# Weight sums of one output product made in earlier pairs, with their loads and stores on ScalarE's queue

## The chip, the cores and the metric

The kernel runs on 1 core of one Trainium2 chip. Times are device microseconds (us) of one execution. The times before are three runs, 1965.34, 1966.95 and 1966.96 us, median 1966.95 us. The engines are named as in the profile: PE (TensorE matmuls) and PEld (its weight loads), DVE (VectorE), ACT (ScalarE), POOL (GpSimd) and SP (SyncE, which here only issues DMAs).

## The reference

One decoder layer over 512 tokens of width 2048, all in float32. The change touches the weights of the output product `mix @ w_out`.

```python
h = rms_norm(x, norm1_g)
proj = h @ w_in                                   # 2048 x 6160
qa, ka, va, ra, ga, qb, kb, vb = split(proj)
out_a = gla_mixer(qa, ka, va, ra, log_g(ga), onorm_g)      # 4 heads
out_b = dilated_mixer(norm(qb), norm(kb), vb, rel_bias)    # 8 heads
mix = concatenate([out_a, out_b])
x = x + mix @ w_out                               # 2048 x 2048
h2 = rms_norm(x, norm2_g)
x = x + (silu(h2 @ w_gate) * (h2 @ w_up)) @ w_down
```

## The kernel before

Every large product is made by a scheme with seven multiplications in place of eight (Strassen-Winograd) on 2 x 2 blocks. A **pair** is two blocks of 512 output columns that are made together. A pair runs through seven products in the order P1, P5, P6, P3, P7, P2, P4, each over four groups g0 to g3 of 512 input rows. One product of one group is an **item**, so a pair has 28 items. The weights of a group come as four quarters a, b, c, d of 256 rows x 512 columns (512 KB each, `load_quarter`, line 222). P1, P3 and P2 take a, d and c as they are. P5, P6, P7 and P4 take the differences b-a, d-a, d-b and c-a (with the a of that moment), which DVE makes in place (`Pair.source`, line 256): 16 sums of 128 x 1024 in a pair.

In an item, ACT rounds the weights to the high part `wh` (line 331, a "cast"), DVE makes the remainder `wl` (line 335), and PE multiplies: eight matmuls with `wh`, four with `wl` (line 367, 128x512 each). Two buffers each hold `wh` and `wl`, and twelve (`wpool`) hold quarters, so ACT can be at most one item ahead of PE.

The order of the pairs: a hand-ordered first pair (lines 435 and before, columns qa and ka); then `pairs[0]` (va), `pairs[1]` (qb0, kb0), `pairs[2]` (vb), `pairs[3]` (qb1, kb1), `pairs[4]` (the gate), two pairs of the output product (here **out(0)** and out(1)), eleven pairs of gate and up, six of down. The mixers run as background generators, which `p.step()` advances once per item. The left operands of out(0) (`AA`, `AS` in the trace, made at lines 174, 175 and 1251 to 1255) come out of the mixers only while the gate pair and out(0) already run. At the end of the gate pair, line 1178 makes the last gated values (`cr`), which PE transposes at line 1129.

All loads and stores are issued on SP's queue, but for three small ones on ACT's queue at the start. In `pairs[0]` SP also issues line 628, the load `rep_d<-bias_d`, which repeats the bias tables in memory: 2560 KB in one DMA.

Only the first pair is recorded under `tc.manual_schedule(engines=ordered)`. For all that comes after, the framework sorts each engine's instructions by itself, so an instruction's place on its engine is not the place where the source calls it. Each engine then works through its queue in that order, and an instruction that waits holds all behind it. Each DMA of SP and ACT gets one of eight completion counters in turn, and is issued only when the DMA before it on the same counter has landed.

Of the kernel before, what the change touches and what calls it, by code (L numbers as in the profile page):

```python
# [10 lines left out]
F32 = mybir.dt.float32  # L11
# [3 lines left out]
ALU = mybir.AluOpType  # L15
# [3 lines left out]
P = 128  # L19
# [14 lines left out]
SINGLE = {"P1": "a", "P3": "d", "P2": "c"}  # L34
SUMS_OF = {"P5": "ba", "P6": "da", "P7": "db", "P4": "ca"}
# [72 lines left out]
def block_kernel(ctx: ExitStack, tc: tile.TileContext, ins, out):  # L108
    nc = tc.nc
    x, w_in, w_out, w_gate, w_up, w_down = (  # L110
        ins[n] for n in ("x", "w_in", "w_out", "w_gate", "w_up", "w_down")
    )
# [33 lines left out]
    load = nc.sync.dma_start  # L146
# [89 lines left out]
    class Pair:  # L236


        def __init__(self, op, rows, w1, w2, final, step, scale=None, before=None):
            self.op, self.rows, self.w1, self.w2 = op, rows, w1, w2  # L240
            self.final, self.step, self.scale, self.before = final, step, scale, before
            self.q, self.dst, self.held = {}, {}, {}

        def quarter(self, name, g):
# [5 lines left out]
        def source(self, prod, g):  # L250

            if prod in SINGLE:
                return self.quarter(SINGLE[prod], g)
            one, two = SUMS_OF[prod]
            src = self.quarter(two, g)
            nc.vector.tensor_tensor(src, self.quarter(one, g), src, op=ALU.subtract)  # L256
            return src
# [50 lines left out]
        def end(self, prod):  # L308
            src = self.dst[prod]
            if prod in ("P1", "P5", "P6"):  # L310
                self.held[prod] = self.seeds(src, int(prod == "P5"))
            elif prod == "P4":
                later(1, lambda: self.final(1, 0, None, src), hold=True)
            else:
                which = {"P3": "P6", "P7": "P5", "P2": "P1"}[prod]
                self.close(self.held[which], src, *CLOSES[prod])

    def stream(pairs):

# [184 lines left out]
    def later(units, fn, hold=False):  # L504

        deferred.append([units, fn, hold])
# [20 lines left out]
    def finish(ready):  # L527

        tries = 0
        while not ready():  # L530
            tries += 1
            assert tries < 100
            run_soon()
            try:
                next(background[0])
            except StopIteration:
                background.pop(0)

    def paced(counts):
        counts = iter(counts)  # L540
        return lambda: step(next(counts, 1))

    def rate(*stretches):


        owed = [0.0]
        rates = iter([r for n, r in stretches for _ in range(n)])

        def go():
            owed[0] += next(rates, stretches[-1][1])  # L550
            n = owed[0] if owed[0] > 0.3 else 0
            owed[0] = min(owed[0] - (step(n) or 0.0), 1.0)

        return go
# [79 lines left out]
    row_scale = lambda half, m: rs1[:, 2 * half + m : 2 * half + m + 1]  # L634
# [464 lines left out]
    order = (2, 3, 0, 1)  # L1099

    def final_proj(n1, n2):
        def final(half, which, tiles, acc_):
            if tiles is None:
                tiles = emitted(acc_, lambda m: row_scale(half, m))
            name = (n1, n2)[which]
            dst = proj[name]
            for m in range(2):
                r = half * 256 + m * P
                put = lambda r=r, m=m: store(dst[r : r + P, :], tiles[m])
                if name[:2] in ("qb", "kb"):  # L1110
# [183 lines left out]
    opm = Operand(4)  # L1294
    pairs = []

    def pair(*args, **kw):
        pairs.append(Pair(*args, **kw))

    pair(opx, rows_in, col(1536), col(1024), final_proj("va1", "va0"), rate((22, 1), (6, 0.6)),  # L1300
         row_scale, before=lambda: background.extend([gates(), bias_tables()]))
    flow = rate((90, 0.41))
    pair(opx, rows_in, col(3088), col(4112), final_proj("qb0", "kb0"), flow, row_scale)
    pair(opx, rows_in, col(5648), col(5136), final_proj("vb1", "vb0"), flow, row_scale)
    pair(opx, rows_in, col(3600), col(4624), final_proj("qb1", "kb1"), flow, row_scale)
    pair(opx, rows_in, col(2048), col(2560), final_gate, rate((5, 0.6), (23, 1.05)), row_scale)


    rows_mix = [(1024 + 256 * g, 256 * order[g]) for g in range(4)]
# [36 lines left out]
    def final_out(second):  # L1346
        rest_of = {}

        def ahead(half, which):
            tok = 1 - half  # L1350
            rest_of[half, which] = residual_loads(
                [2 * tok, 2 * tok + 1], 512 * (2 * second + which),
                lambda t, c: x[t * P : (t + 1) * P, c : c + 512],
            )

        def final(half, which, tiles, acc_):
            tok = 1 - half
            rows = [2 * tok, 2 * tok + 1]
            ch = 2 * second + which
            tiles = residual(tiles, acc_, rest_of.pop((half, which)))  # L1360
            for m in range(2):
                t = rows[m]
                store(x1_d[t][:, 512 * ch : 512 * ch + 512], tiles[m])
                jk = work("st", (P, DV), bufs=2).bitcast(mybir.dt.bfloat16)
                nc.scalar.activation(
                    jk, tiles[m], AF.Square, accum_out=ss2[:, t, ch : ch + 1]
                )
            if second:
                turn = scaled_store(tiles, rows, tok, xn_d[2 * ch : 2 * ch + 2], 4 * ch)

                def rest():
                    turn()
                    if which == 1 and half == 1:
                        background.append(early_jobs(opn, (2, 3), tops, False))
                        background.append(late_jobs(opn, ((2, 3),), tops, bots, False))

                later(2, rest)
                if which == 0 and half == 1:
                    output_scales()
            elif which == 0 and half == 1:  # L1380
                nc.vector.tensor_tensor(part2, ss2[:, :, 0], ss2[:, :, 1], op=ALU.add)
# [35 lines left out]
        turn()  # L1417
        yield

    ocol = lambda c: w_out[:, c : c + 512]  # L1420
# [98 lines left out]
    for j in range(11):  # L1519
        c = slice(512 * j, 512 * j + 512)  # L1520
# [32 lines left out]
    for i in range(3):  # L1553
        g0 = 4 * i
        rows_d = [(512 * (g0 + g), 512 * (g0 + g) + 256) for g in range(opd[i].groups)]
        for np_ in range(2):
            c = 1024 * np_
# [4 lines left out]
                before=(lambda i=i: background.append(down_jobs(i + 1))) if lead else None,  # L1562
# [46 lines left out]
```

## Time and profile before

| | |
|---|---|
| runs | 1965.34, 1966.95, 1966.96 us, median 1966.95 |
| profiled execution, its own time | 1968.84 us |
| its span in the profile | 1967.1 us |
| PE busy | 1927.6 us (98%) |
| DVE busy | 1653.7 us (84%) |
| ACT busy | 1093.8 us (56%) |
| DMA queue q1 (SP) | 358.72 MB, 57.6% of 16 engines |

The page gives busy time by engine, the span in 40 slices, the DMA queues, the chain of work that ended last, and groups of like instructions. A row of the timeline gives the start in us, the duration, engine and line, the tiles written and read, how many instructions it merges, and in brackets the idle time before it and who ended it. A row of the windows gives a stretch, its length, busy us of PE, PEld, DVE, ACT and POOL, the granted TensorE clock, the share of the DMA engines in use, and GB/s.

### The profile page before, as it was taken

To read this page: it belongs to the slowest core of one execution; us is meant where nothing else is said; L and a number is where in the kernel's file an instruction comes from. 1 tells how busy PE (TensorE), PEld (TensorE's weight loads), DVE (VectorE), ACT (ScalarE), POOL (GpSimd) and SP (SyncE) were. 2 spreads that over 40 slices of the span, in tenths; PEclk is the share of its full clock that TensorE was granted. 3 is DMA by queue.
4 is the path that set the end of the run, shared out by engine and by line. 5 is a ranking of instruction groups with operands and counts; after the bars stand their busy time and mean duration, and the time that the engine had idled before them with its cause. 6 is when DMAs were issued, how large, how long until landed. Compare 5 with 4: busy or idle time off the path is not lost.

```text
span 1967.1 us, 25785 instructions
## 1 busy us (share of the span) xinstructions
PE 1927.6 (98%) x9226; PEld 1670.9 (85%) x9226; DVE 1653.7 (84%) x1850; ACT 1093.8 (56%) x1600; POOL 60.9 (3%) x81
## 2 busy tenths in 40 slices
PE   8999999999999999999999999999999999999998
PEld 7888888888878877888888888888888888888887
DVE  8997787868789889878878878878879989989987
ACT  8554564566766766545545445545446646546443
POOL 0000230010000000000000000000000000000000
PEclk9999999999999999999999999999999999999999
DMA  8447455463766684554554553554555865855662
GB/s 278 141 162 266 119 171 170 134 200 124 221 213 202 215 288 152 177 167 133 178 170 127 179 163 127 176 164 130 172 163 168 299 203 185 310 183 175 236 214 75
DMA packets 237114, 360.45 MB, mean 183 GB/s; under 512 B 18246, under 2 KB 96783, under 8 KB 236984
## 3 DMA queue, kind: packets, MB, share of 16 engines
q1 hardware_dynamic: 236776, 358.72, 57.6%
q8 instruction: 72, 1.18, 0.3%
q14 instruction: 58, 0.48, 0.1%
q10 hardware_dynamic: 208, 0.08, 0.0%
HBM read 296.59 MB, written 64.51 MB: 184 GB/s over the span
## 4 chain that ended last, share of the span: by engine, by line
PE 75%; DVE 8%; DMA 5%; issue 3%; ACT 2%; POOL 0%; SPq 0%; DVEq 0%; ACTq 0%
PE acc L367 71%; DVE wl L335 3%; DVE wa L256 2%; PE bank L1129 1%; DVE AS L175 1%; PE bank L987 1%; DMA q<-in_x 1%; DMA xn_d<-oT 1%; ACT wh L331 1%; DMA q<-y_d 0%; DVE seed L294 0%; PE bank L1019 0%; DVE seed L1334 0%; DMA r<-xn_d 0%; DMA wc<-in_w_down 0%
## 5 line engine op out<-in xcount | busy, mean ns | idle before, releaser
L367 PE MATMUL acc<-wh,AS 128*128 128x512 f32 x3008 | 712.5, 380 | 0.6 <-ACT wh L331 0.5
L367 PEld LDWEIGHTS acc<-wh,AS 128*128 128x128 f32 x3008 | 569.8, 190 | 82.3 <-ACT wh L331 1.8
L331 ACT CAST wh<-wa 128x1024 fp32r<-128x1024 f32 x376 | 394.0, 1048 | 392.4 <-PE acc L367 363.0
L367 PE MATMUL acc<-wh,AA 128*128 128x512 f32 x2256 | 535.0, 380 | 0.0
L335 DVE TENSOR_TENSOR wl<-wa,wh 128x1024 fp32r<-128x1024 f32 x376 | 456.3, 1217 | 69.2 <-ACT wh L331 43.6
L367 PEld LDWEIGHTS acc<-wh,AA 128*128 128x128 f32 x2256 | 427.4, 190 | 61.4 <-ACT wh L331 0.9
L367 PE MATMUL acc<-wl,AS 128*128 128x512 f32 x1504 | 395.3, 385 | 9.7 <-DVE wl L335 9.5
L367 PEld LDWEIGHTS acc<-wl,AS 128*128 128x128 f32 x1504 | 279.4, 189 | 62.0 <-DVE wl L335 21.0
L367 PE MATMUL acc<-wl,AA 128*128 128x512 f32 x1128 | 298.1, 387 | 7.9 <-DVE wl L335 7.7
L367 PEld LDWEIGHTS acc<-wl,AA 128*128 128x128 f32 x1128 | 209.6, 190 | 41.5 <-DVE wl L335 12.4
L331 ACT CAST wh<-wb 128x1024 fp32r<-128x1024 f32 x94 | 98.5, 1049 | 129.7 <-PE acc L367 127.8
L331 ACT CAST wh<-wc 128x1024 fp32r<-128x1024 f32 x94 | 98.4, 1047 | 111.5 <-PE acc L367 101.7
L331 ACT CAST wh<-wd 128x1024 fp32r<-128x1024 f32 x94 | 98.5, 1048 | 105.8 <-PE acc L367 102.3
L256 DVE TENSOR_TENSOR wa<-wc,wa 128x1024 f32<-128x1024 f32 x94 | 114.4, 1221 | 46.2 <-DMA wc<-in_w_gate 25.1
L335 DVE TENSOR_TENSOR wl<-wc,wh 128x1024 fp32r<-128x1024 f32 x94 | 114.5, 1218 | 35.6 <-ACT wh L331 35.6
L335 DVE TENSOR_TENSOR wl<-wd,wh 128x1024 fp32r<-128x1024 f32 x94 | 114.3, 1219 | 34.9 <-ACT wh L331 28.2
L335 DVE TENSOR_TENSOR wl<-wb,wh 128x1024 fp32r<-128x1024 f32 x94 | 113.6, 1216 | 5.5 <-ACT wh L331 5.5
L256 DVE TENSOR_TENSOR wb<-wd,wb 128x1024 f32<-128x1024 f32 x94 | 114.3, 1216 | 1.1 <-DMA wd<-in_w_in 0.6
L256 DVE TENSOR_TENSOR wa<-wb,wa 128x1024 f32<-128x1024 f32 x94 | 113.6, 1218 | 0.8
L256 DVE TENSOR_TENSOR wa<-wd,wa 128x1024 f32<-128x1024 f32 x94 | 112.8, 1215 | 0.1
L298 DVE SCALAR_TENSOR_TENSOR seed<-acc,rs,seed 128x512 f32<-128x512 f32 x96 | 70.4, 745 | 24.9 <-PE acc L367 24.9
L282 ACT ACTIVATE seed<-acc,rs 128x512 f32<-128x512 f32 x96 | 60.6, 681 | 1.4 <-PE acc L367 0.8
(303 smaller groups left out, 1365.1 us busy)
## 6 DMA issues: line engine op xcount, KB each, us to landing
wa<-in_w_gate SPq DMA_DIRECT2D x44, 512.0 KB, 3.9
wb<-in_w_up SPq DMA_DIRECT2D x44, 512.0 KB, 4.3
wd<-in_w_up SPq DMA_DIRECT2D x44, 512.0 KB, 4.3
wc<-in_w_gate SPq DMA_DIRECT2D x44, 512.0 KB, 3.7
wc<-in_w_in SPq DMA_DIRECT2D x28, 512.0 KB, 3.9
wa<-in_w_in SPq DMA_DIRECT2D x24, 512.0 KB, 5.1
wb<-in_w_in SPq DMA_DIRECT2D x24, 512.0 KB, 6.0
wd<-in_w_in SPq DMA_DIRECT2D x24, 512.0 KB, 5.9
```

What stands on the lines that cost most here:

```text
L175: nc.vector.tensor_tensor(a[:, :, 1, :], src, a[:, :, 0, :].bitcast(F32), op=ALU.subtract)
L256: nc.vector.tensor_tensor(src, self.quarter(one, g), src, op=ALU.subtract)
L282: nc.scalar.activation(halves(t), unfolded(src[m]), AF.Copy, scale=self.scale(half, m))
L298: nc.vector.scalar_tensor_tensor(halves(seed[m]), unfolded(src[m]), self.scale(half, m), halves(seed[m]), op0=ALU.mult, op1=ALU.add,)
L331: nc.scalar.copy(high[k], sources[k])
L335: nc.vector.tensor_tensor(low[k], sources.pop(k), high[k].bitcast(F32), op=ALU.subtract)
L367: nc.tensor.matmul(p.dst[prod][m], a[:, jj, hl, m * P : (m + 1) * P], folded(w[:, jj, :]), start=fresh and g == 0 and len(terms) == 2 and ...
L987: nc.tensor.matmul(lp[:, :n], qh[:, b * P : (b + 1) * P], kh[:, :n], start=True, stop=True)
L1129: nc.tensor.transpose(bk[:, jj, m * P : (m + 1) * P], tiles[m][:, f : f + P], ident)
```

## The change

The 16 sums of out(0) are no longer made in out(0). A generator `weight_sums` makes them in `pairs[0]` to `pairs[2]` in eight blocks (group g, half j): four loads of 128 x 512 (256 KB) from `w_out` into `rpool` (four buffers), four sums of 128 x 512 on DVE, and four stores of 256 KB into DRAM tiles `P5_g_d`, `P7_g_d`, `P6_g_d`, `P4_g_d`. Loads and stores are issued by `nc.scalar.dma_start`, that is on ACT's queue. `beside` advances the plan one step per item; a block starts every nine items from item 12 on. In out(0), `source` loads a finished sum (512 KB, tile `ws`) with SP, so that out(0) has 28 loads of 512 KB instead of 16.

```diff
         def source(self, prod, g):
 
             if prod in SINGLE:
-                return self.quarter(SINGLE[prod], g)
+                t = self.quarter(SINGLE[prod], g)
+                if self.sums:
+                    self.q.pop((SINGLE[prod], g))
+                return t
+            if self.sums:
+                t = wpool.tile([P, 2, 512], F32, name=nm("ws"), tag="w")
+                load(t, self.sums[prod, g])
+                return t
...
+    def weight_sums(rows, w1, w2, sums):
+        tt = nc.vector.tensor_tensor
+        plan = {}
+
+        def at(group, fn):
+            plan.setdefault(group, []).append(fn)
+
+        def block(start, g, j):
+            t = {}
+
+            def fetch(name):
+                r0 = rows[g][0 if name in "ab" else 1] + P * j
+                t[name] = rpool.tile([P, 512], F32, name=nm("r"), tag="r")
+                nc.scalar.dma_start(t[name], (w1 if name in "ac" else w2)[r0 : r0 + P, :])
+
+            def less(dst, one, two):
+                tt(t[dst], t[one], t[two], op=ALU.subtract)
+
+            def put(prod, name):
+                nc.scalar.dma_start(sums[prod, g][:, j, :], t[name])
+
+            at(start, lambda: fetch("a"))
+            at(start, lambda: fetch("b"))
+            at(start + 1, lambda: fetch("d"))
+            at(start + 2, lambda: fetch("c"))
+            for i, (dst, one, two, prod) in enumerate(
+                (("a", "b", "a", "P5"), ("b", "d", "b", "P7"), ("d", "d", "a", "P6"),
+                 ("c", "c", "d", "P4"))
+            ):
+                at(start + 4 + i, lambda dst=dst, one=one, two=two: less(dst, one, two))
+                at(start + 5 + i, lambda prod=prod, dst=dst: put(prod, dst))
+
+        for i in range(8):
+            block(12 + 9 * i, i // 2, i % 2)
+        for n in range(max(plan) + 1):
+            for fn in plan.get(n, ()):
+                fn()
+            yield
...
+    early_sums = weight_sums(rows_mix, ocol(0), ocol(512), out_sums)
+    pair(opx, rows_in, col(1536), col(1024), final_proj("va1", "va0"),
+         beside(rate((22, 1), (6, 0.6)), early_sums),
          row_scale, before=lambda: background.extend([gates(), bias_tables()]))
     flow = rate((90, 0.41))
+    flowing = beside(flow, early_sums)
-    pair(opx, rows_in, col(3088), col(4112), final_proj("qb0", "kb0"), flow, row_scale)
-    pair(opx, rows_in, col(5648), col(5136), final_proj("vb1", "vb0"), flow, row_scale)
+    pair(opx, rows_in, col(3088), col(4112), final_proj("qb0", "kb0"), flowing, row_scale)
+    pair(opx, rows_in, col(5648), col(5136), final_proj("vb1", "vb0"), flowing, row_scale)
...
-    pair(opm, rows_mix, ocol(0), ocol(512), final_out(0), paced([1] * 28))
+    pair(opm, rows_mix, ocol(0), ocol(512), final_out(0), paced([1] * 28), sums=out_sums)
```

The changed program, as built, has this order of instructions in `pairs[0]` (st and ld are DMA stores and loads of the plan, the number in brackets is the block, and each line is in order on its queue):

```
ACT  cast P3 g3 | st P6(0), ld a(1), ld b(1) | cast P7 g0 | st P4(0), ld d(1) | cast P7 g1 | ld c(1)
     cast P7 g2 | st P5(1) | cast P7 g3 | st P7(1), st P6(1), ld a(2) | cast P2 g0 | st P4(1), ld b(2)
     cast P2 g1 | ld d(2), ld c(2) | cast P2 g2
     st P5 P7 P6 P4 (2), ld a b d c (3), st P5 P7 P6 P4 (3), ld a b d c (4), ... , st P5 P7 P6 P4 (7)
     cast P2 g3 | cast P4 g0 ...
DVE  wl P2 g1 | sums 1, 2 of (2) | wl P2 g2 | sums 3, 4 of (2) | the 20 sums of (3) to (7)
     weight sum of P4 g3 | wl P2 g3 ...
SP   rep_d | va store, va store, load c of P2 g3 ("wc"), va store, va store, T load, T load, v load | loads of pairs[1]
```

Waits in it that the dependencies of the data do not show: st P6(1) has the counter of `rep_d`; the two va stores, the wc load and the next va store on SP have the counters of ld a(7), b(7), d(7) and c(7). A load of a block goes into the buffer whose store of the block before must have landed (a after P5, b after P7, d after P6, c after P4). In `pairs[1]` to `pairs[4]` the order on every engine is that of before. In out(0) the remaining instructions of DVE, ACT and SP are sorted anew.

More of the change, by code (lines that the diff above doesn't have):

```diff
@@ L236, in block_kernel, with __init__ @@
     class Pair:
-        def __init__(self, op, rows, w1, w2, final, step, scale=None, before=None):
+        def __init__(self, op, rows, w1, w2, final, step, scale=None, before=None, sums=None):
             self.op, self.rows, self.w1, self.w2 = op, rows, w1, w2
             self.final, self.step, self.scale, self.before = final, step, scale, before
+            self.sums = sums
             self.q, self.dst, self.held = {}, {}, {}
@@ L537, in finish, with beside, both @@
                 background.pop(0)
+    def beside(go, gen):
+        def both():
+            go()
+            next(gen, None)
+        return both
     def paced(counts):
@@ L1298, in pair @@
         pairs.append(Pair(*args, **kw))
-    pair(opx, rows_in, col(1536), col(1024), final_proj("va1", "va0"), rate((22, 1), (6, 0.6)),
+    ocol = lambda c: w_out[:, c : c + 512]
+    rows_mix = [(1024 + 256 * g, 256 * order[g]) for g in range(4)]
+    out_sums = {
+        (prod, g): dram([P, 2, 512], f"{prod}_{g}_d") for prod in SUMS_OF for g in range(4)
+    }
+    early_sums = weight_sums(rows_mix, ocol(0), ocol(512), out_sums)
+    pair(opx, rows_in, col(1536), col(1024), final_proj("va1", "va0"),
+         beside(rate((22, 1), (6, 0.6)), early_sums),
          row_scale, before=lambda: background.extend([gates(), bias_tables()]))
     flow = rate((90, 0.41))
-    pair(opx, rows_in, col(3088), col(4112), final_proj("qb0", "kb0"), flow, row_scale)
-    pair(opx, rows_in, col(5648), col(5136), final_proj("vb1", "vb0"), flow, row_scale)
+    flowing = beside(flow, early_sums)
+    pair(opx, rows_in, col(3088), col(4112), final_proj("qb0", "kb0"), flowing, row_scale)
+    pair(opx, rows_in, col(5648), col(5136), final_proj("vb1", "vb0"), flowing, row_scale)
     pair(opx, rows_in, col(3600), col(4624), final_proj("qb1", "kb1"), flow, row_scale)
     pair(opx, rows_in, col(2048), col(2560), final_gate, rate((5, 0.6), (23, 1.05)), row_scale)
-    rows_mix = [(1024 + 256 * g, 256 * order[g]) for g in range(4)]
     x1_d = [dram([P, D], f"x1_d{t}") for t in range(4)]
@@ L1418, in first_columns @@
         yield
-    ocol = lambda c: w_out[:, c : c + 512]
     def output_scales():
```

## Prediction

> **What bounds the kernel now.** I read the page's head first, then the windows, then the timeline of PE and DVE in the stage that the change relieves, then that of ACT, PE and SP in the stage that it loads.
>
> ```profile
> span 1967.1 us, 25785 instructions
> PE 1927.6 (98%) x9226; PEld 1670.9 (85%) x9226; DVE 1653.7 (84%) x1850; ACT 1093.8 (56%) x1600; POOL 60.9 (3%) x81
> ```
>
> PE is the bound, with 39.5 us of idle time in the whole span. Less work on DVE gains only where PE waits for DVE. Two windows and the timeline show that out(0) is such a place.
>
> ```profile
> 500.00:600.00 100.00, 90.90 (x464) 76.05 (x462) 79.17 (x121) 65.93 (x121) 0.00 (x0) 0.98 0.66 206
> 570.00:580.00 10.00, 7.92 (x31) 6.50 (x32) 8.86 (x13) 8.57 (x15) 0.00 (x0) 0.83 0.59 187
> ```
> ```profile
> 559.20 1.04 PE L1129 MATMUL bank<-mats,seed 128*128 128x128 f32 x8
> ...
> 560.93 1.89 PE L367 MATMUL acc<-wh,AA 128*128 128x512 f32 x8
> ...
> 570.11 1.13 PE L367 MATMUL acc<-wl,AA 128*128 128x512 f32 x4 [1.40 <-DVE wl L335]
> 573.05 0.44 PE L1129 MATMUL bank<-mats,cr 128*128 128x128 f32 x2 [1.81 <-DVE cr L1178]
> ...
> 574.84 3.02 PE L367 MATMUL acc<-wh,AA 128*128 128x512 f32 x8
> ...
> 578.57 1.89 PE L367 MATMUL acc<-wh,AS 128*128 128x512 f32 x8
> ...
> 604.05 1.89 PE L367 MATMUL acc<-wh,AS 128*128 128x512 f32 x8
> ...
> 645.50 1.89 PE L367 MATMUL acc<-wh,AA 128*128 128x512 f32 x8
> ```
>
> out(0) begins at 560.93. Its items 1 to 4 (P1) reach to 578.57, items 5 to 12 (P5, P6) to 604.05, and the last 16 to 645.50. The last 16 take 41.45 us, 2.59 each, without loss. At that pace P5 and P6 would take 20.7 us and not 25.48 (4.8 lost). P1 takes 17.64 where four items (10.4) and eight transposes of line 1129 (1.04 for such eight at 559.20) need 11.4: 6.2 lost. So 11.0 us can be won in out(0), and no more. What PE waits for there is DVE:
>
> ```profile
> 562.17 1.23 DVE L256 TENSOR_TENSOR wa<-wb,wa 128x1024 f32<-128x1024 f32 x1
> 563.43 1.23 DVE L256 TENSOR_TENSOR wb<-wd,wb 128x1024 f32<-128x1024 f32 x1
> ...
> 570.57 1.22 DVE L256 TENSOR_TENSOR wa<-wb,wa 128x1024 f32<-128x1024 f32 x1
> 571.70 0.69 DVE L1253 TENSOR_TENSOR r<-r,qT 128x512 f32<-128x512 f32 x1
> 572.30 1.29 DVE L1178 TENSOR_TENSOR cr<-cr,og 128x512 f32<-128x512 f32 x2
> ...
> 580.11 1.22 DVE L256 TENSOR_TENSOR wa<-wb,wa 128x1024 f32<-128x1024 f32 x1
> 581.24 0.68 DVE L175 TENSOR_TENSOR AS<-r,AS 128x512 fp32r<-128x512 f32 x1
> 581.85 1.22 DVE L335 TENSOR_TENSOR wl<-wa,wh 128x1024 fp32r<-128x1024 f32 x1
> 582.98 0.68 DVE L1251 TENSOR_TENSOR r<-PT,r 128x512 f32<-128x512 f32 x1
> 583.58 1.22 DVE L256 TENSOR_TENSOR wa<-wb,wa 128x1024 f32<-128x1024 f32 x1
> ```
>
> **What is removed.** An item of P5 or P6 costs DVE 3.47 us (580.11 to 583.58), PE 2.59. Without the weight sum (1.13 from start to start) it costs DVE 2.34, under PE's pace, and the 4.8 us can go. In P1 three sums stand ahead of `cr`; without them (3.4 us) the waits of 1.40 and 1.81 can go, and with them the half clock behind the second (0.83 over 10 us is 1.7 us of clock; one item's matmuls take 3.02, not 1.89). I take 4.8 + 2.2 = **7 us gained**, between 3 (ACT's new order puts operand casts that wait for loads ahead of weight casts, and twelve more loads of 512 KB, 6.3 MB, join a stage that moves 206 GB/s) and 11 (all). The other eight sums, of P7 and P4, lie beside PE and are worth nothing.
>
> **What is added, and where the built order puts it.** The source spreads eight blocks over 75 items. The built order does not: 24 sums (blocks 2 to 7) stand on DVE around and behind the remainder of P2 g2 of `pairs[0]`, and on ACT 24 stores and 20 loads stand between the casts of P2 g2 and P2 g3. With four buffers a block cannot load before the block before it is stored, so ACT and DVE, and behind them PE, stand still for five rounds of store, load and sum. This part carries the result; its rows:
>
> ```profile
> 141.23 0.72 SPq L628 DMA_DIRECT2D rep_d<-bias_d  x1
> ...
> 149.91 0.43 SPq L222 DMA_DIRECT2D wc<-in_w_in  x1
> ```
> ```profile
> 153.07 1.05 ACT L331 CAST wh<-wc 128x1024 fp32r<-128x1024 f32 x1 [1.54 <-PE acc L367]
> ...
> 161.17 1.05 ACT L331 CAST wh<-wc 128x1024 fp32r<-128x1024 f32 x1 [1.87 <-DMA wc<-in_w_in]
> ```
> ```profile
> 156.32 1.89 PE L367 MATMUL acc<-wh,AA 128*128 128x512 f32 x8
> ...
> 164.54 0.59 PE L367 MATMUL acc<-wh,AA 128*128 128x512 f32 x2
> ```
> ```profile
> 144.00:148.00 4.00, 4.00 (x20) 3.50 (x19) 3.30 (x4) 1.16 (x2) 0.00 (x0) 1.00 0.50 198
> 154.00:158.00 4.00, 4.00 (x20) 3.52 (x19) 2.92 (x3) 1.17 (x2) 0.00 (x0) 1.00 0.54 206
> ```
>
> 153.07 is the cast of P2 g0, 161.17 that of P2 g3; PE begins these items at 156.32 and 164.54.
>
> *Blocks 0 and 1* lie between casts one at a time. A sum of 128x512 is 0.68 (582.98), and DVE and ACT have the slack for it: nothing, as long as no store or load keeps ACT longer than a cast's slack; the 64 issues on ACT, 0.4 us each by SP's rows, lie in this slack or in the stops below, and POOL's queue is untouched. That slack is 156.32 - 154.12 = 2.2 us.
>
> *First stop.* Store P6 of block 1 stands ahead of the cast of P2 g0 and waits until `rep_d` has landed. `rep_d` is issued at 141.23, and half of the DMA engines then move about 206 GB/s until 158: 2560 KB at that rate are 12.7 us, so I estimate its landing at 158 to 159 before (the wc load issued behind it at 149.91 keeps ACT until 161.17). Now it is issued some 1 us later (two sums of 0.68 ahead of the bias copies on DVE) and shares the engines with about five transfers of block 1, half of whose 1.3 MB costs up to 3.2 us at 206 GB/s: 159 to 163, taken 161.5. With two issues the cast comes at 162.2 and not 153.07; less the slack of 2.2, PE begins P2 g0 6.9 us late (4.5 to 8.5), at **163.2**. The Trainium skill, DMA: Bandwidth & Descriptors, section "Issuing engines are not separate DMA queues", speaks against the change here: DMAs of several engines run on the same 16 DMA engines and interleave, and a second issuer saves only issue time. By that rule the ACT transfers cannot pass by `rep_d`, which is the upper end of this term, 163, and 1.5 us more in the sum; no trace here shows two queues at work at once.
>
> *The rounds.* PE then has items g0, g1 and g2, 7.8 us, and runs dry at 171. In that time block 2 loads and sums; its fourth sum I put at 170.5 (cast ends 163.2, store P4(1) 2.4 and load c 3.1 bring 168.7, and 1.8 for what of two sums and a remainder comes behind). Then come five rounds. In each, the last store must land before load c, and load c before the last sum:
>
> ```profile
> 668.57 2.42 DMA xn_d<-oT
> 670.99 0.02 issue
> 671.01 3.09 DMA r<-xn_d
> ```
> ```profile
> S_d<-r SPq DMA_DIRECT2D x44, 256.0 KB, 2.0
> T<-x_d SPq DMA_DIRECT2D x4, 256.0 KB, 3.0
> r<-p_d SPq DMA_DIRECT2D x44, 256.0 KB, 3.6
> out<-seed SPq DMA_DIRECT2D x12, 256.0 KB, 4.1
> wc<-in_w_in SPq DMA_DIRECT2D x28, 512.0 KB, 3.9
> ```
>
> The chain at 668.57 is just such a store and load of 256 KB: 2.42 + 3.09, and with the sum 6.2. A round moves 2.1 MB in eight transfers, so I add 0.6 for sharing: **6.8 a round**, 34 us in five, to 204.5. The lower bound is 2.0 + 3.0 + 0.68 = 5.7 (28.5 in five), the upper 4.1 + 3.6 + 0.68 = 8.4 (42).
>
> *After the last round* P2 g3 still lacks its weights: on SP the wc load stands behind va stores that wait for block 7's loads, and itself waits for ld d(7), which I put at 203.2. It lands 3.9 later, with the two va stores beside it 4.7, at 207.9; the cast (1.05) brings PE to 209.0, against 164.54. **Delay 44.5 us.** What comes behind on SP (va, T, v and the first loads of `pairs[1]`) is needed 10 us later or more, and the buffers are long free, so I count it at nothing; if PE must wait for the T load too, 1 us.
>
> *The clock.* Before, a wait of 1.81 us was followed by 1.7 us of lost clock (the 570 to 580 window). The long stop will be followed by one such loss: **1.7 us**. The first stop's loss falls into time in which PE runs dry anyway. The Trainium skill, TensorE: Matmul & The Clock Gate, "What's actually happening", says that the clock halves after an idle window of some 3.4 us and comes back after 3.4 us of work; by that the wait of 1.81 us would not have halved it, so the trace goes further than the rule. By the rule each stop costs 1.7, and the sum would be up to 1.7 higher.
>
> **Sum:** 44.5 + 1.7 - 7 = +39.2 us on the profiled execution, 1968.84 (span 1967.1): 2008.0. That execution is 1.9 us above the median of the runs, 1966.95, so the forecast for a median is 1966.95 + 39.2 = **2006 us**.
>
> **Rivals.**
> - *Faster (chance 0.03).* The plan works as the source is written: a store waits for a sum long made, ACT passes it in an issue of about 0.4 us, and only the gain is left: 1967 - 7 = 1960. It needs the stores and loads between two casts to cost ACT under the 2.2 us of slack, a third of one round. Against it: five rounds stand there. What speaks for it is only that no trace here shows this queue under load.
> - *No change, 1967 (0.01).* The stops happen to give back just the gain.
> - *The sharing is worse (0.12).* If eight transfers of a round land as slowly as the slowest group above, and more, a round is 9 to 10 us: five are 45 to 50, and the time 2017 to 2022. For it: `rep_d` may reach into the first rounds. Against it: while PE stands, SP's loads of weights stand too.
> - *The gain does not come (0.10).* The change does not do what it says in out(0): the `ws` loads or the operand casts on ACT take the place of the DVE waits. The gain is 0 and the time 2013.
> - *A short stop (0.09).* `rep_d` lands before ACT asks (-6.9) and rounds take the lowest rows (-5.5): 1994.
>
> **How the numbers follow.** The forecast has 0.65. The bounds give 39.2 - 5.5 - 2.4 - 4 = 27 (1994) and 39.2 + 8 + 1.6 + 2.7 + 4 = 55.5 (2022); with the rivals beside them I take 1991 to 2026. A measurement tells apart about 0.2%, 4 us. Faster by over that 0.03, within it 0.01, slower 0.96.
>
> **What would show it.** PE with one hole of about 35 us and a smaller one ahead of it, between 155 and 215, in `pairs[0]`, DVE and ACT nearly empty in it; DVE's `r<-r` sums in groups of four at 6 to 8 us; ACT's queue with groups of four stores and four loads between two casts; PEclk under 1 behind the hole. From `pairs[1]` on, stages of the same length as before, and out(0) shorter by 3 to 11 us, with P5 and P6 at 2.59 an item. The forecast is wrong if ACT's casts of `pairs[0]` keep their pace, if the sums are spread over three pairs, or if out(0) gets longer.

## The result, and the profile after

| | before | after |
|---|---|---|
| median of 4 runs each, us | 1966.87 | 2023.85 (2021.71 to 2027.21) |
| ratio, 95% interval | | 1.0286 [1.0273, 1.0298] |
| profiled execution, its own time | 1968.84 | 2021.71 |
| its span | 1967.1 | 2019.6 |

The change made the kernel 57 us slower; the two profiled executions, which the terms below are taken from, differ by 52.9, for that of before was the slowest of its kernel and that of after the fastest of its four. The page of the changed kernel says where to look:

```profile
span 2019.6 us, 25944 instructions
...
PE 1932.7 (96%) x9226; PEld 1671.7 (83%) x9226; DVE 1657.7 (82%) x1866; ACT 1094.3 (54%) x1600; POOL 61.1 (3%) x81
...
PE   8993599999999998999999999999999999999998
...
PEclk9997799999999999999999999999999999999999
...
L416 PE MATMUL acc<-wh,AA 128*128 128x512 f32 x2256 | 538.0, 381 | 53.3 <-ACT wh L380 53.2
```

Hardly any engine has more work (PE 5 us, DVE 4). PE's busy share shows one dent, in the slices from 150 to 250 us, and the idle time that is new stands in one group: 53.2 us in which PE waited for casts of ACT. The timeline of ACT around that place (start, duration, engine and line, tiles, count, and in brackets the idle time before and who ended it):

```profile
153.21 0.33 ACTq L341 DMA_DIRECT2D r<-in_w_out  x1
153.64 1.05 ACT L380 CAST wh<-wb 128x1024 fp32r<-128x1024 f32 x1 [4.14 <-DVE seed L306]
...
156.58 9.07 ACTq L347 DMA_DIRECT2D P_d<-r  x2
...
166.22 1.04 ACT L380 CAST wh<-wc 128x1024 fp32r<-128x1024 f32 x1 [10.59 <-DMA rep_d<-bias_d]
...
172.05 4.88 ACTq L347 DMA_DIRECT2D P_d<-r  x4
176.97 2.29 ACTq L341 DMA_DIRECT2D r<-in_w_out  x4
183.09 2.51 ACTq L347 DMA_DIRECT2D P_d<-r  x4
185.69 2.07 ACTq L341 DMA_DIRECT2D r<-in_w_out  x4
...
217.61 3.30 ACTq L347 DMA_DIRECT2D P_d<-r  x4
222.55 1.05 ACT L380 CAST wh<-wc 128x1024 fp32r<-128x1024 f32 x1 [50.37 <-DMA wc<-in_w_in]
```

Both stops can be read here. Two stores of block 1 keep the queue for 9.07 us, and the bracket of the cast behind them names `rep_d`. Then fours of stores and fours of loads follow each other for 50 us with no cast among them. On DVE the sums of the blocks stand in groups of four, and SP's load of P2 g3's weights comes behind all of it:

```profile
175.16 1.41 DVE L344 TENSOR_TENSOR r<-r,r 128x512 f32<-128x512 f32 x2
182.36 2.87 DVE L344 TENSOR_TENSOR r<-r,r 128x512 f32<-128x512 f32 x4 [5.79 <-DMA r<-in_w_out]
190.00 0.69 DVE L344 TENSOR_TENSOR r<-r,r 128x512 f32<-128x512 f32 x1 [4.77 <-DMA r<-in_w_out]
190.86 2.14 DVE L344 TENSOR_TENSOR r<-r,r 128x512 f32<-128x512 f32 x3 [0.16 <-DMA r<-in_w_out]
...
216.88 2.87 DVE L344 TENSOR_TENSOR r<-r,r 128x512 f32<-128x512 f32 x4 [6.69 <-DMA va<-seed]
```
```profile
143.70 0.72 SPq L686 DMA_DIRECT2D rep_d<-bias_d  x1
...
217.56 0.39 SPq L222 DMA_DIRECT2D wc<-in_w_in  x1
```

PE's own rows, first around the two stops and then in out(0):

```profile
167.32 3.78 PE L416 MATMUL acc<-wh,AA 128*128 128x512 f32 x8 [7.13 <-ACT wh L380]
170.90 1.91 PE L416 MATMUL acc<-wl,AA 128*128 128x512 f32 x4
172.60 2.03 PE L416 MATMUL acc<-wh,AA 128*128 128x512 f32 x8
...
223.65 1.22 PE L416 MATMUL acc<-wh,AA 128*128 128x512 f32 x2 [45.12 <-ACT wh L380]
226.22 1.24 PE L909 MATMUL bank<-mats,T 128*128 128x128 f32 x4 [1.35 <-DMA T<-ls_d]
...
228.18 3.20 PE L416 MATMUL acc<-wh,AA 128*128 128x512 f32 x6
...
232.08 1.89 PE L416 MATMUL acc<-wh,AA 128*128 128x512 f32 x8
...
623.89 1.89 PE L416 MATMUL acc<-wh,AA 128*128 128x512 f32 x8
...
639.13 1.89 PE L416 MATMUL acc<-wh,AS 128*128 128x512 f32 x8
...
659.85 1.89 PE L416 MATMUL acc<-wh,AS 128*128 128x512 f32 x8
...
701.80 1.89 PE L416 MATMUL acc<-wh,AA 128*128 128x512 f32 x8
```

P2 g0 begins at 167.32 (before 156.32) and P2 g3 at 223.65 (before 164.54). The last four rows are the beginnings of out(0), of its P5, of its P3, and of out(1): P5 and P6 now take 20.72 us for eight items, 2.59 each, and P1 takes 15.24.

How late the changed kernel is can be followed cast by cast. The table gives, for every kernel told of here, the start of the same cast of ACT less its start in the profile of before, in us, at the beginning of six stages and of the last pair. For the row "after", the first entry is 242.15 - 178.50. Each row is one execution, and it can lie some us off the median of its kernel: that of `gain` was the slowest of its four, that of `ordgps` the fastest of its eleven, 5 us under the median.

| kernel | pairs[1] | pairs[2] | pairs[3] | out(0) | out(1) | first gate and up pair | last pair |
|---|---|---|---|---|---|---|---|
| after | 63.6 | 64.7 | 64.7 | 63.0 | 56.3 | 53.3 | 52.9 |
| gain | 0.4 | 0.0 | 0.0 | -0.7 | -3.6 | -6.3 | -6.7 |
| cost | 62.4 | 63.0 | 63.0 | 61.1 | 61.5 | 60.6 | 59.7 |
| nost | 36.1 | 36.5 | 36.5 | 35.3 | 28.6 | 25.3 | 25.4 |
| order | 4.0 | 7.0 | 8.6 | 6.1 | -0.4 | -0.8 | -0.4 |
| ordcost | 7.2 | 10.0 | 11.7 | 8.9 | 9.4 | 8.7 | 6.9 |
| ordnosum | 6.7 | 8.4 | 9.5 | 8.2 | 2.8 | -0.3 | -1.3 |
| ordlate | 0.8 | 17.3 | 26.5 | 25.1 | 19.3 | 16.7 | 14.9 |
| ordpool | 7.4 | 17.9 | 25.4 | 21.9 | 16.5 | 13.5 | 12.8 |
| ordpoollate | -0.1 | 23.0 | 34.7 | 33.4 | 27.2 | 24.2 | 24.8 |
| gaps | 3.4 | 11.2 | 13.7 | 11.1 | 6.2 | 2.8 | 2.7 |
| ordgps | 4.2 | 8.4 | 9.3 | 7.1 | 0.3 | -3.4 | -4.1 |
| gapsgps | 3.0 | 11.0 | 14.7 | 13.4 | 7.2 | 3.9 | 2.4 |

### The profile page after: what moved, and what is told of

Same layout as the page of the kernel before. It is cut to its first block, busy times and chain, and to the rows that moved or that the text cites. A ratio compares the mean times of both kernels' runs of the same rounds, so it can differ in the third digit from the quotient of the medians.

```text
span 2019.6 us, 25944 instructions
## 1 busy us (share of the span) xinstructions
PE 1932.7 (96%) x9226; PEld 1671.7 (83%) x9226; DVE 1657.7 (82%) x1866; ACT 1094.3 (54%) x1600; POOL 61.1 (3%) x81
## 4 chain that ended last, share of the span: by engine, by line
PE 77%; DMA 9%; DVE 7%; issue 3%; ACT 2%; SPq 1%; POOL 0%; ACTq 0%; DVEq 0%
PE acc L416 70%; DVE wl L384 2%; PE acc L484 2%; DMA r<-in_w_out 2%; DMA rep_d<-bias_d 1%; DVE wa L264 1%; DMA k<-y_d 1%; PE bank L1187 1%; PE bank L1045 1%; ACT wh L380 1%; DVE r L344 1%; PE bank L1077 1%; DMA x<-in_x 1%; DMA mix_d<-r 0%; DMA xn_d<-oT 0%
## 5 line engine op out<-in xcount | busy, mean ns | idle before, releaser
L380 ACT CAST wh<-wa 128x1024 fp32r<-128x1024 f32 x364 | 381.5, 1049 | 388.6 <-PE acc L416 356.2
L416 PE MATMUL acc<-wh,AA 128*128 128x512 f32 x2256 | 538.0, 381 | 53.3 <-ACT wh L380 53.2
L384 DVE TENSOR_TENSOR wl<-wa,wh 128x1024 fp32r<-128x1024 f32 x364 | 441.6, 1217 | 68.7 <-ACT wh L380 43.6
L380 ACT CAST wh<-wb 128x1024 fp32r<-128x1024 f32 x90 | 94.2, 1049 | 126.7 <-PE acc L416 121.0
L264 DVE TENSOR_TENSOR wa<-wc,wa 128x1024 f32<-128x1024 f32 x90 | 109.6, 1221 | 46.7 <-DMA wc<-in_w_gate 23.9
L384 DVE TENSOR_TENSOR wl<-wb,wh 128x1024 fp32r<-128x1024 f32 x90 | 108.8, 1216 | 5.3 <-ACT wh L380 5.1
L264 DVE TENSOR_TENSOR wb<-wd,wb 128x1024 f32<-128x1024 f32 x90 | 109.4, 1216 | 1.7 <-DMA wd<-in_w_in 1.2
L264 DVE TENSOR_TENSOR wa<-wb,wa 128x1024 f32<-128x1024 f32 x90 | 108.6, 1218 | 0.7
L264 DVE TENSOR_TENSOR wa<-wd,wa 128x1024 f32<-128x1024 f32 x90 | 108.0, 1214 | 0.1
L290 ACT ACTIVATE seed<-acc,rs 128x512 f32<-128x512 f32 x96 | 60.6, 681 | 1.9 <-PE acc L416 1.3
```

What stands on the lines that cost most here:

```text
L290: nc.scalar.activation(halves(t), unfolded(src[m]), AF.Copy, scale=self.scale(half, m))
L380: nc.scalar.copy(high[k], sources[k])
L384: nc.vector.tensor_tensor(low[k], sources.pop(k), high[k].bitcast(F32), op=ALU.subtract)
L416: nc.tensor.matmul(p.dst[prod][m], a[:, jj, hl, m * P : (m + 1) * P], folded(w[:, jj, :]), start=fresh and g == 0 and len(terms) == 2 and ...
```

## The experiments

**Gain and cost apart.** Two kernels split the change. In `gain` nothing is made early:

```diff
-                load(t, self.sums[prod, g])
+                one = SUMS_OF[prod][0]
+                r0 = self.rows[g][0 if one in "ab" else 1]
+                v = self.w1 if one in "ac" else self.w2
+                load(t, v[r0 : r0 + 256, :].rearrange("(j p) n -> p j n", p=P))
...
-         beside(rate((22, 1), (6, 0.6)), early_sums),
+         rate((22, 1), (6, 0.6)),
...
-    flowing = beside(flow, early_sums)
+    flowing = flow
```

> No sums are made early; the first half of the output product loads a raw quarter of w_out wherever the changed kernel loads a finished sum (the subtraction of two quarters is left out of the result). This measures the gain alone. My theory (the gain is real and lies in the first half of the output product, the loss is the order in the second pair): 7 us under the kernel before by the prediction's term, so about 1960; by the trace after, in which the delay falls by 11 to 12 us from the third pair to the end, about 1955.5. Rival (nothing to gain, the delay is lost elsewhere): 1967 within 2.

Measured: 1957.88 us against 1967.76, ratio 0.9946 [0.9930, 0.9963]. The gain is real, 9.9 us by the medians (the profiled execution shows 6.7 at the last pair). In `cost` the sums are made and not used:

```diff
-    pair(opm, rows_mix, ocol(0), ocol(512), final_out(0), paced([1] * 28), sums=out_sums)
+    pair(opm, rows_mix, ocol(0), ocol(512), final_out(0), paced([1] * 28))
```

> The sums are made and stored as in the changed kernel, but the first half of the output product takes its quarters and subtracts as before; the stored sums are read by nobody. This measures the cost alone. My theory: the delay of 64.7 us that stands in the trace after at the third pair stays to the end: 1967 + 64.7 = 2031.6, within 3. Rival (part of the fall of the delay behind the third pair has nothing to do with the sums that are loaded, but is slack that takes up any delay): nearer 2024.

Measured: 2028.77 us, ratio 1.0308 [1.0293, 1.0324], 61 us over before and within 3 of what the theory gave. In the table its delay stays near 61 where that of the changed kernel falls by 9.7 from out(0) to the end of out(1). Only the 2 us that go in the gate pair go here too: these are slack, no gain.

**The order alone.** `order` does all the work and all the transfers of the change, but ties each step of the plan to its place:

```diff
         def first_part(k):
-            nc.scalar.copy(high[k], sources[k])
+            recent["act"] = nc.scalar.copy(high[k], sources[k]).ins
...
-            nc.vector.tensor_tensor(
+            recent["dve"] = nc.vector.tensor_tensor(
                 low[k], sources.pop(k), high[k].bitcast(F32), op=ALU.subtract
-            )
+            ).ins
...
             go()
-            next(gen, None)
+            with tc.issue_after(recent["act"]), tc.issue_after(recent["dve"]):
+                next(gen, None)
```

> The same loads, subtractions and stores, each step of the plan queued on its engine behind the last cast of its group, so that they stand spread over three pairs and not in one hole between two casts. My theory (the order in the queue of ScalarE makes the loss, and neither the work of VectorE nor the traffic does): the hole of 59 us goes, and what is left is the gain and a few waits of ScalarE behind completion counters: 1956 to 1966, the middle 1960. Rival A (the subtractions and 8 MB of traffic themselves cost, wherever they stand): over 1985. Rival B (each group's store holds the next cast up by its wait on a transfer, a loss of some 1 us in each of 64 places): near 2010.

Measured: 1967.34 us, ratio 1.0000 [0.9991, 1.0010]. The hole is gone with the same instructions in another order, so rival A and the work itself are out as causes of the 57 us, and the 2010 of rival B did not come. The edit ties ACT and DVE at once, so it does not say which of the two orders weighs more. The time is above the 1956 to 1966 of the forecast, 7 us over its middle: the spread plan still makes the kernel 8.6 us late behind the fourth pair, which takes the gain up. ACT and SP of `order` show half of that:

```profile
158.95 1.05 ACT L380 CAST wh<-wc 128x1024 fp32r<-128x1024 f32 x1 [1.54 <-PE acc L416]
159.03 0.82 ACTq L341 DMA_DIRECT2D r<-in_w_out  x2
167.27 1.04 ACT L380 CAST wh<-wc 128x1024 fp32r<-128x1024 f32 x1 [7.26 <-DMA T<-ls_d]
```
```profile
160.96 0.32 SPq L1168 DMA_DIRECT2D va<-seed  x1
161.37 0.39 SPq L222 DMA_DIRECT2D wc<-in_w_in  x1
```

The first two rows of ACT are the cast of P2 g2 and the loads behind it, the third is the cast of P2 g3. The va store ahead of the wc load now has `rep_d`'s counter: SP waits 11.7 us for `rep_d` there. So the load is issued at 161.37 (before at 149.91), and the cast of P2 g3 comes at 167.27 (before 161.17). The bracket of this cast names a T load, which came last by the profile; that it waited for the wc load is read from the order.

**What a round is made of.** `nost` is the change without its stores, with loads and sums still in the same hole:

```diff
                 at(start + 4 + i, lambda dst=dst, one=one, two=two: less(dst, one, two))
-                at(start + 5 + i, lambda prod=prod, dst=dst: put(prod, dst))
```

> The plan without its stores: loads and subtractions stand in the same hole, 20 loads between the same two casts of ScalarE (the first half of the output product loads a raw quarter in place of each sum; the finished sums are dropped). This tells what a round of 8.6 us is made of. If it is the chain store landed, load issued, load landed, sum: the round loses the store's part and is about 4 to 5 us, the loss in the second pair some 20 us smaller or more, the time 1990 to 2003. If it is the subtractions of VectorE or the loads that set the round: still near 8 us, 2018 or more. The first stop, before the third group set's first cast, would go as well if a store waiting behind the bias table's broadcast makes it, some 10 us: then 1985 to 1995.

Measured: 1996.03 us, ratio 1.0143 [1.0128, 1.0158]. Its ACT and DVE:

```profile
154.77 1.04 ACT L382 CAST wh<-wc 128x1024 fp32r<-128x1024 f32 x1 [1.84 <-PE acc L418]
...
164.88 28.65 ACTq L344 DMA_DIRECT2D r<-in_w_out  x20
195.09 1.04 ACT L382 CAST wh<-wc 128x1024 fp32r<-128x1024 f32 x1 [34.40 <-DMA va<-seed]
```
```profile
165.90 1.41 DVE L347 TENSOR_TENSOR r<-r,r 128x512 f32<-128x512 f32 x2
170.02 0.69 DVE L347 TENSOR_TENSOR r<-r,r 128x512 f32<-128x512 f32 x1 [2.71 <-DMA r<-in_w_out]
171.14 2.14 DVE L347 TENSOR_TENSOR r<-r,r 128x512 f32<-128x512 f32 x3 [0.43 <-DMA r<-in_w_out]
...
197.04 2.87 DVE L347 TENSOR_TENSOR r<-r,r 128x512 f32<-128x512 f32 x4 [4.36 <-DMA r<-in_w_out]
```

The cast of P2 g0 comes at 154.77 with 1.84 us of idle time before it: the first stop is gone with the stores. Five rounds reach from 167.31 (165.90 + 1.41) to 199.91 (197.04 + 2.87), 6.5 each. The time is within the chain theory's range of 1990 to 2003, and 1 us over the 1985 to 1995 given for the case that the first stop goes too. Its round of 4 to 5 us was too short: loads and sums alone take 6.5, and the stores add 2.1 to reach 8.6.

**What the spread plan costs.** `ordcost` is `order` with out(0) as before (the same one line as in `cost`).

> The spread plan of the run order, with the first half of the output product subtracting as before: the cost of the spread work alone. In the trace of order, TensorE's casts are 8.6 us late behind the fourth pair and the delay falls again by 9 to 10 in the two halves of the output product, which is why order ended at the time before. If both are real, this is 1967.8 + 8.6 = 1976, within 2. Rival (the spread plan costs nothing that lasts, and it is the gain that was lost in order): 1968 to 1970.

Measured: 1975.43 us, ratio 1.0043 [1.0028, 1.0058], 7.9 us over before, as expected. `order` is thus a gain of 8 us on a cost of 8. Then I tried to be rid of this cost. `ordlate` moves the plan, in `order`, past the broadcast:

```diff
-            block(12 + 9 * i, i // 2, i % 2)
+            block(29 + 6 * i, i // 2, i % 2)
```

> As order, but the plan begins in the third pair (a block every 6 groups from group 29 on, all within the third and fourth pair), past the broadcast of the bias table, behind whose counter the va stores and with them a weight load stood in order (a stop of 3 us of TensorE, 4 us of the delay). My theory (waits behind completion counters and crowded transfers, not the 22 us of subtractions): those 4 us go, 1960 to 1965, the middle 1963. Rival (VectorE has no room for 22 us of subtractions in three pairs, and less in two): the waits of TensorE for the low parts grow, 1967 or more.

Measured: 1984.21 us, ratio 1.0088 [1.0073, 1.0103]. My theory gave 1963 and fell. The first stop did go (0.8 us late at the third pair, where `order` is 4.0 late), but the two pairs that now hold eight blocks lost 26 us. Two places of its ACT:

```profile
260.41 1.05 ACT L380 CAST wh<-wc 128x1024 fp32r<-128x1024 f32 x1 [3.43 <-DVE seed L306]
...
265.96 0.34 ACTq L341 DMA_DIRECT2D r<-in_w_out  x1
266.35 0.31 ACT L1136 ACTIVATE jk<-seed 128x128 bf16<-128x128 f32 x1 [4.59 <-DMA P_d<-r]
...
266.66 1.03 ACT L380 CAST wh<-wc 128x1024 fp32r<-128x1024 f32 x1
...
352.35 2.67 ACTq L341 DMA_DIRECT2D r<-in_w_out  x2
355.11 1.04 ACT L380 CAST wh<-wb 128x1024 fp32r<-128x1024 f32 x1 [4.89 <-DMA P_d<-r]
```

A load waits for the store of the block before, which must first free its buffer, and the next cast waits behind that load. With a block every six groups, the next block's loads are due while the last stores are being issued. It is the same chain as in the hole, in small pieces. The rival's sign, longer waits for `wl`, is there as well: from 178 to 455 us PE waits 8.5 us for casts and 8.5 for `wl`, in `order` none and 4.6. So this run does not part the pace of the blocks from DVE's lack of room; for the pace speaks `gaps` below, whose blocks in the same pairs stand 9 to 10 groups apart and which loses 10.3 us there for six blocks, where `ordlate` loses 25.7 for eight.

`ordpool` gives the subtractions to GpSimd (`nc.gpsimd.tensor_tensor`, each step queued behind the last cast and GpSimd's last instruction); `ordpoollate` does this on `ordlate`.

> As order, but the 32 subtractions are GpSimd's and not VectorE's, each behind the last instruction that GpSimd had before it. In order, TensorE waited 6.3 us for low parts of VectorE in the second to fourth pair, against 2.8 before. If the subtractions make that: about 3.5 us less, 1962 to 1965. If it is the transfers (va stores and weight loads behind completion counters) as my theory has it: 1966 to 1968, for the first stop stays.

> Both at once: begun in the third pair, subtractions on GpSimd. If counters and VectorE's order each take a part of the 8.6 us: 1957 to 1961, the best of all. If GpSimd's slower subtractions hold the stores on ScalarE's queue and so its casts: over 1968.

Measured: 1980.69 us, ratio 1.0069 [1.0054, 1.0084], and 1991.12 us, 1.0120 [1.0103, 1.0137]. The first is outside what both of its theories gave; the second is the case of slow sums. Groups of GpSimd in `ordpool` and of DVE in `order`, both from the second to the fourth pair:

```profile
L344 POOL TENSOR_TENSOR r<-r,r 128x512 f32<-128x512 f32 x32 | 55.8, 1743 | 76.8 <-DMA r<-in_w_out 69.7 <-issue 5.8
```
```profile
L344 DVE TENSOR_TENSOR r<-r,r 128x512 f32<-128x512 f32 x32 | 21.9, 684 | 0.0
```

A sum takes 1743 ns there and 684 ns on DVE, 2.5 times as long, and what stands behind it on ACT's queue comes later: from 95 to 460 us ACT's casts waited 19.5 us for sums of GpSimd, against 4.3 for the sums of DVE in `order`. Nor did DVE win room. Its own steps became slower: `wa<-wc` took 1426 ns in place of 1224 in this window, `wl<-wa` 1312 in place of 1218, and over the whole span DVE was busy for 1657.5 us, against 1654.9 in `order` with the 22 us of sums. So these two runs do not test a DVE that is rid of the sums; `ordnosum` below does. The Trainium skill, GPSIMD Engine Reference, section "3.1 Elementwise — side-by-side cycle accounting", gives 1.96 times for an add of 2048 elements; at 512 elements this kernel paid more.

`gaps` is `order` with the blocks 9 to 10 groups apart, none beside the broadcast, and each sum one group earlier; `ordgps` is `order` with the stores on GpSimd's queue (each behind GpSimd's last instruction there); `gapsgps` is both:

```diff
-            block(12 + 9 * i, i // 2, i % 2)
+            block((0, 9, 28, 38, 48, 57, 66, 75)[i], i // 2, i % 2)
...
-                at(start + 4 + i, lambda dst=dst, one=one, two=two: less(dst, one, two))
+                at(start + 3 + i, lambda dst=dst, one=one, two=two: less(dst, one, two))
...
-                nc.scalar.dma_start(sums[prod, g][:, j, :], t[name])
+                nc.gpsimd.dma_start(sums[prod, g][:, j, :], t[name])
```

> As order, with another plan: two blocks at the start of the second pair (groups 0 and 9 of it), none beside the broadcast of the bias table, six from group 28 on, 9 to 10 groups apart, and each sum one group sooner after its loads, so that a store on ScalarE's queue waits less for its sum. The run ordlate spoke against the broadcast as what matters and for the pace: with a block every 6 groups, loads waited for the stores that freed their buffers. My theory now (the waits of ScalarE's loads and stores in its queue, by their pace, make the 8 us that order lost): the delay behind the fourth pair falls from 8.6 to 2 to 5 us, the time 1960 to 1964. Rival (8 MB more traffic and 22 us more of VectorE cost 8 us wherever they stand): 1966 to 1969.

> As order, but the 32 stores are issued on GpSimd's queue, so that none of ScalarE's casts or small activations stands behind a store that waits for a sum of VectorE. If the stores on ScalarE's queue make most of the 8 us that order lost: 1960 to 1964. If the subtractions and the traffic make it: 1966 to 1969. If GpSimd's own small steps (which VectorE waits for) now stand behind stores: over 1970.

> Both: the plan of the run gaps and the stores on GpSimd's queue. If both reasons hold, 1957.5 to 1961, which is the 10 us of gain with next to none of it lost; if only one of them, the better one of the other two.

Measured: 1969.68 us, ratio 1.0011 [1.0001, 1.0021]; 1968.95 us, 1.0009 [1.0000, 1.0019]; 1971.57 us, 1.0022 [1.0013, 1.0031]. None of the three gave the time that I hoped for. `ordgps` fell to its rival of 1966 to 1969 and `gaps` came out just above the same rival; `gapsgps` is outside all that was foretold, worse than either of the other two. In `gaps` the first stop is gone, and the third pair loses 7.8 us in its place (3.4 to 11.2 in the table): PE waits 4.0 us for `wl` and 1.7 for casts there. No version that makes the sums early beat the kernel before.

**Sums or transfers.** The last run takes the subtractions out of `order` and leaves every load and store where it was:

```diff
-                at(start + 4 + i, lambda dst=dst, one=one, two=two: less(dst, one, two))
```

> The run order without its 32 subtractions: the loads and stores stand at the same places on ScalarE's queue, and each store writes the loaded block as it came (the sums of the first half of the output product are left out of the result). What is still open is whether the 8 us that the spread plan costs in the second to fourth pair (7.7 in the run ordcost) are VectorE's 22 us of subtractions or the 64 transfers and their waits. If VectorE's: the delay behind the fourth pair is 0 to 3 us in place of 8.6, and the time 1959 to 1961. If the transfers': it stays at 7 to 9 us, 1965 to 1968. The stop of 3 us behind the bias table's broadcast, which the transfers make, would stay in either case and makes 1962 to 1963 the likeliest.

Measured: 1966.94 us, ratio 1.0004 [0.9993, 1.0014]. PE's groups from 95 to 460 us, first `order`, then `ordnosum` (after the bar: busy us and mean ns, then idle us and who ended it):

```profile
L416 PE MATMUL acc<-wh,AA 128*128 128x512 f32 x392 | 93.3, 380 | 3.0 <-ACT wh L380 3.0
L416 PE MATMUL acc<-wl,AS 128*128 128x512 f32 x256 | 70.0, 396 | 3.8 <-DVE wl L384 3.7
L416 PE MATMUL acc<-wl,AA 128*128 128x512 f32 x192 | 52.4, 395 | 2.6 <-DVE wl L384 2.6
```
```profile
L415 PE MATMUL acc<-wh,AA 128*128 128x512 f32 x392 | 93.8, 382 | 3.2 <-ACT wh L379 3.2
L415 PE MATMUL acc<-wl,AS 128*128 128x512 f32 x256 | 70.1, 396 | 3.4 <-DVE wl L383 3.4
L415 PE MATMUL acc<-wl,AA 128*128 128x512 f32 x192 | 52.4, 395 | 1.2 <-DVE wl L383 1.2
```

Without 22 us of DVE's work, PE waits 1.7 us less for `wl`, and neither the delay behind the fourth pair (9.5, first cast of `pairs[3]`) nor the time is less. Within the 2 us that the interval leaves, the 64 transfers and what waits behind them make the spread plan's cost, not the subtractions; the stop of 3 us stays, as expected (3.2 us for casts). Whether it is their place in the queues or the traffic itself is open: three ways to place them left the sum where it was.

## Why the prediction was right in kind and short in size

The mechanism was the one foretold: two stops in `pairs[0]`, groups of four stores and four loads between two casts, and out(0) shorter. `order` shows that the order of these instructions makes the loss. The forecast of 2006 us was 18 short, and the time lies inside the range of 1991 to 2026, near its upper end. Of the 18, the terms below account for 13.7, in us of the profiles; the other 4.1 are the two profiled executions, 1.9 above the median before and 2.1 below it after. The delay was 18.5 short (64.7 for 46.2), and a larger gain hid 4.8 of that: the time lies so near by some luck.

| step | predicted | measured |
|---|---|---|
| PE begins P2 g0 | +6.9 (163.2) | +11.0 (167.32) |
| fourth sum of block 2 | 170.5 | 176.57 |
| five rounds | 34 (6.8 each) | 43.2 (8.6 each) |
| from there to PE's P2 g3 | 4.5 | 3.9 |
| delay at P2 g3 | 44.5 | 59.1 |
| behind it, to the end of the third pair | 1.7 | 5.6 |
| gain | -7 | -11.8 |
| sum | +39.2 | +52.9 |

- *First stop.* The cause was right: `nost`, without stores, has none. The size was short twice. PE came to it 3.7 us late already (the item before begins at 157.43, before at 153.73), of which 1.0 stood at the start of `pairs[0]`, ahead of the plan's first step. ACT stood before a load of block 1 until 153.21 (cast at 153.64, against 147.89 for the same one before; what the load waited for stays open, the bracket names a step of DVE); I had counted blocks 0 and 1 at nothing. And `rep_d`, issued at 143.70, held its waiter until about 165.3 (156.58 + 9.07, less an issue of 0.33), not 161.5. The working for 161.5 had a gap: 12.7 us from 141.23 on end at 153.9, and the 158 to 159 that I started from rested on the cast at 161.17 alone. The rule of the Trainium skill weighed in the prediction (DMA: Bandwidth & Descriptors, "Issuing engines are not separate DMA queues"), that transfers of several issuers interleave on the same engines, pointed to this side, and 165.3 lies beyond even the 163 that stood beside it; no run shows how much of it is sharing.
- *The rounds* are the largest miss, 9.2 us. The step that was mis-sized is "load c before the last sum", which put one sum of 0.68 behind the last load. The rows show all four there: ACT has its last load out at 179.26 (176.97 + 2.29), the sums begin at 182.36 and run 2.87. The four loads land close together, so that the first sum can hardly start before the last load is in. Four sums for one are 2.2 us, and with them the 6.8 would have been 9.0. The rival of worse sharing (9 to 10 us a round) had a nearer size by another reason: stores landed in 2.1 us (median over the hole), no slower than in the quoted rows.
- *After the hole* PE ran at half clock longer than one wait of 1.81 us had led me to think. (That wait did not stand alone, either: only 1.13 us of work lay between it and a wait of 1.40, so the rows of before do not show that 1.81 us by themselves halve the clock.) The rows: 228.18 has six matmuls in 3.20 us, and only at 232.08 are eight in 1.89 again. From 223.65 on, PE was held for 1.35 us by the T load, which I had put at up to 1, and the rest of the 4.5 us up to 232.08 (63.6 late there) is clock, about 3. One more microsecond went before the third pair's end.
- *The gain.* P5 and P6 gave 4.76 (4.8 predicted), and this reading holds everywhere: they last 20.72 us in every kernel here that loads its sums or quarters in their place, and 25.5 in those that subtract in out(0). P1 gave 2.4 (2.2 predicted), but here the number is luck. The prediction did not work its 2.2 out, PE's waits for DVE in P1 did not go (1.63 and 0.90, before 1.40 and 1.81; most of the 2.4 is clock), and in `gain` P1 lasts 18.65, longer than before. The last 16 items took 0.5 more than before. I missed out(1), which gave 3.0 more though "no more" than out(0) was to be won, and about 2 in the gate pair, which are slack that takes up a part of any delay. By the medians the gain is 9.9 us alone (`gain`), 8.1 in `order` against `ordcost`, and 4.9 in the change against `cost` (6.8 in the table); why it is less there stays open.
- *Faster, by a plan that works as written.* The prediction put 1960 on it. `order` is that plan, and it gives 1967: even spread, store and load queues cost what the gain brings.

## What to carry to other kernels

Before costing work that "runs beside", read the order in which it was built: 32 loads and 32 stores in few buffers cost 61 us with most of them between two casts (`cost`), and 8 when each was tied to its place (`ordcost`). Where loads, work and stores go around through few buffers, a round is store, load and all the work that waits for the last load, not its last piece. And even a spread plan is not free on a queue that feeds the bound engine: here 64 transfers cost the 8 us that they were meant to win, with or without the arithmetic between them.

## What the hardware showed that was not expected

- Half clock can outlast a stop by more than the stop before had shown. After 7.13 us of idle time PE needed from 167.32 to about 172.9 of steady work to be back at full clock (eight matmuls in 3.78 us, then in 2.03; granted clock 0.50 from 164 to 172 and 0.89 from 172 to 176); after 45.12 us it took until about 231 (0.50 from 222 to 230, 0.89 from 230 to 234). The Trainium skill, TensorE: Matmul & The Clock Gate, "What's actually happening", has a free-running window of some 3.4 us that must be busy; work that begins within one such window could wait for the end of the next, 6.8 us by my estimate, and the 5.6 us of the first stop lie within that. The loss there, (3.78 - 1.89) + (1.91 - 1.03) = 2.8 us, is more than the 1.7 that the prediction took from one wait.
- A small DMA can be held for some 8 to 12 us by a large one it has nothing to do with, through the completion counter that both use: two stores of 256 KB took ACT's queue from 156.58 to 165.65 because one had the counter of a broadcast of 2560 KB (8.4 us of it are the wait), and in `order` the same broadcast held a va store, and the weight load behind it on SP, for 11.7 us.
- The same subtraction of 128x512 took 684 ns on DVE and 1743 ns on GpSimd, and while GpSimd made them, DVE's own subtractions of 128x1024 took 1426 ns (`wa<-wc`) where they took 1224 without.
